# A fused attention and retention block on one core: parts of h by VectorE alone, reloads and stores at other steps

## The chip, the core and the metric

The kernel runs on one core of a Trainium2 chip. Its engines are TensorE (PE in the profile; PEld is its loading of weights), VectorE (DVE), ScalarE (ACT), GpSimd (POOL) and SyncE (SP), which only issues DMAs. ScalarE and GpSimd issue DMAs too, from their own queues. Each engine works off its instructions in the order of the program. The metric is device time in microseconds of one execution.

## The reference

One layer of an encoder over 512 positions and 2048 channels, all in float32. Cut to what matters here:

```
h    = rmsnorm(x) * norm_gain
proj = h @ w_in          # split into aq ak av az | iq ik iw | rq rk rv rz | ga gb
sel  = top 256 of relu(iq . ik) weighted by iw, per query, chunk-causal
a    = softmax(aq . ak[sel] * s + bias[bucket(pos)]) @ av[sel] * silu(az)
b    = groupnorm(retention(rope(rq), rope(rk), rv)) * silu(rz)
m    = sigmoid(ga) * (a @ w_a_out) + sigmoid(gb) * (b @ w_b_out)
r    = x + m @ w_o
y    = rmsnorm(r + (p @ w_ple) * sigmoid(r @ w_ple_gate)) * final_gain
```

## The kernel before

Every matrix product is made precise by splitting each operand into a high part (a copy to fp32r) and a low part (the rest), and adding three products: high x high, high x low, low x high. For a weight, `split_to` does this: ScalarE writes the high part `wh` (L153) and, one or more steps later, VectorE the low part `wl` (L158). Weights come from HBM into `wraw`, or into one of five big buffers (`wt`), by DMAs on SP's queue (`load_to`, L132), eight units ahead of use; they are split three units ahead.

Most projections are done in pairs with seven products in place of eight (a Strassen-like scheme). It needs sums of weight blocks: the sum of two blocks is made by loading one and letting a second DMA add the other in place (`add_block`, L119; it is issued on GpSimd's queue, and waits there until the buffer may be changed). It also needs sums and differences of the four quarters of h. `combos` makes these: for each of eight k, `xn_norm` scales two tiles of x (L707), `sums` makes four differences of 256 columns (L313 to L316), and `parts` splits each of seven operands into a copy on ScalarE (L299) and a low part (L301, or L303 where the sign is turned). In the kernel before, the four differences and three of the seven low parts (s1, s4, a22) are GpSimd's, the rest VectorE's. Of the first four k, the last three operands (twelve tiles, `x_away`) are stored to HBM (`hd`) and loaded back by `x_load`, as there are not enough tile slots (69) while the plain parts of h are still needed.

Order is written out by hand. `step()` counts steps: one follows each three matmuls in the plain products, and each two in `gemm_pair`. A function can be put off by n steps (`later`), put in line (`todo`), or on a background list (`bg`), of which one entry is run each `rate` steps when nothing else is in line. The background list holds, in this order, the parts of h (a load, a norm and four steps for each k), 48 top-k rounds on VectorE (MAX8 and a replace over 256, 384 or 512 columns, L650 and L651, after the last round of each a mask, L653), and the relative bias: masks on VectorE (L666), two banks of matmuls at a time (`bias_mm`, L677), an eviction on ScalarE (L685) and stores to HBM (L689).

The program runs through: index projections and scores; the retention values rv in two halves of 64 steps (`values`, four accumulators, evicted by ScalarE at the end, L764, and stored from its queue, L892); the attention values in one pair (`values_pair`, seven products of 16 steps: banks v, p, q, r, p, v, p, shown as ps_vv, ps_vp and so on; its results leave through `value_out`, L899, L906); then eight heads of retention, each a pair for rq and rk followed by two pairs for gates; then the pairs for rz, for aq and ak, and for az, attention with the output of branch b beside it, and the output projections.

Of the kernel before, what the change touches and what calls it, by code (L numbers as in the profile page):

```python
# [9 lines left out]
F32 = mybir.dt.float32  # L10
F32R = mybir.dt.float32r
# [24 lines left out]
def block_kernel(tc, xT, pT, posb, posq, w_in, w_v, w_ik, w_a, w_b, w_o, w_ple, w_gate,  # L36
# [4 lines left out]
    with contextlib.ExitStack() as ctx:  # L41
# [29 lines left out]
        raw_tiles = {}  # L71
        unfinished = {}
        state = {"raw": 0, "split": 0, "rate": BG_RATE}
        in_raws, in_big = set(), set()

        def raw(src, k0, nk, cols, plus=None):
            raws.append((src, k0, nk, cols, plus))
# [60 lines left out]
        def split_to(n, lag=1):  # L138
            while state["split"] < min(n, len(units)):
                i = state["split"]  # L140
                load_to(i + 1)
                r, plus, nk, cols = units[i]
                if r in unfinished:
                    unfinished[r]()
                raw = view(raw_tiles[r], nk, cols)
                if i in in_raws:
                    t = wp.tile([128, 2, 512], F32R, name="whl", tag="wraw", bufs=RAW_BUFS)
                    h, l = t[:, 0:1], t[:, 1:2]
                elif nk * cols == L:
# [3 lines left out]
                act.activation(h, raw, AF.Copy)  # L153

                def rest(r=r, plus=plus, l=l, raw=raw, h=h):
                    if unfinished.pop(r, None) is None:
                        return
                    dve.tensor_sub(l, raw, h.bitcast(F32))  # L158
# [129 lines left out]
                if ended[n] == 16 and n in after:  # L288
                    after[n]()

        def combos(lo, hi, name, keep=None, adder=dve, low={}):


            X = {n: [None] * 8 for n in PRODUCTS}
            T = {}

            def parts(n, k, src, sign=1.0):
                t = U(name + n, F32R)
                act.activation(t[:, LO], src, AF.Copy, scale=sign)  # L299
                if sign > 0:  # L300
                    low.get(n, dve).tensor_sub(t[:, HI], src, t[:, LO].bitcast(F32))  # L301
                else:
                    dve.scalar_tensor_tensor(t[:, HI], src, sign, t[:, LO].bitcast(F32), op0=OP.mult, op1=OP.subtract)  # L303
# [318 lines left out]
        def index_tile(m, ix):  # L622
            if m > 1:
                todo.extend(N3)
            for s in range(2):
                for t in range(1, NT):
                    todo.append(lambda s=s, t=t: index_score(2 * m + s, ix[s], t))

        for m in range(2):
            index_tile(m, ix[m])  # L630
        for m in range(2, 8):
# [49 lines left out]
        def bias_out(b, ps):  # L681
            t, gs = b
            ln = 128 * (t + 1)
            e = U("bev")
            act.activation(e[:, :ln * len(gs)], ps[:, :ln * len(gs)], AF.Copy, scale=d_back)  # L685
            for n, g in enumerate(gs):
                dst = bass.AP(tensor=scr.tensor, offset=scr.offset + 16 * (g % 8) * 1280 + TOFF[t],
                              ap=[[1280, 16], [128 * 1280, NH], [1, ln]])
                later(8 + 4 * n, lambda dst=dst, n=n: sp.dma_start(dst, e[:, ln * n:ln * n + ln]))  # L689

        def bias_banks(banks):
            for b, ps in [(b, bias_mm(b)) for b in banks]:
                bias_out(b, ps)

        x_away = [(n, k) for k in range(X_AWAY) for n in PRODUCTS[4:]]
        hd = dp.tile([len(x_away), 128, L], F32, name="hd")
        x_at = {nk: hd[i] for i, nk in enumerate(x_away)}
        xn = {}

        def xn_load(k):  # L700
            for i in (k, k + 8):
                xn[i] = U("xn")
                sp.dma_start(xn[i], xT[:, i, :])

        def xn_norm(k):
            for i in (k, k + 8):
                dve.scalar_tensor_tensor(xn[i], xn[i], ng[:, i:i + 1], R["b"], op0=OP.mult, op1=OP.mult)  # L707

        Xh, h_step = combos(lambda k: xn[k], lambda k: xn[k + 8], "h", lambda n, k: x_at.get((n, k)), pool,
                            {n: pool for n in ("s1", "s4", "a22")})  # L710
        bg.append(lambda: xn_load(0))
        for k in range(8):
            if k < 7:
                bg.append(lambda k=k: xn_load(k + 1))
            bg.append(lambda k=k: xn_norm(k))
            bg.extend([lambda k=k, i=i: h_step(k, i) for i in range(X_STEPS)])

        bg.append(lambda: state.update(rate=BG_RATES[1]))
        for r in range(16):
            for t in range(1, NT):  # L720
                bg.append(lambda r=r, t=t: topk_round(t, r == 15))
        bg.append(lambda: state.update(rate=BG_RATES[4]))
# [170 lines left out]
        state["rate"] = BG_RATES[2]  # L893


        def value_out(i, t, f, x, y):

            a = U("av")
            f(a, x, y)  # L899
            if t == NT - 1:  # L900
                vs = [(6, a)]
            else:
                h, l = split(a, "av", 2)
                vs = [(2 * t, h.bitcast(F32)), (2 * t + 1, l.bitcast(F32))]
            for j, v in vs:
                later(10 + 2 * (j % 2), lambda j=j, v=v: act.dma_start(vd[i, j], v))  # L906

        def values_pair(ids):
            banks = {}
# [4 lines left out]
                for j in range(2):  # L914
                    act.activation(E[n][j], banks[b][j], AF.Copy)

            def out(f, b, n, i, half):
                for j in range(2):
                    value_out(i, 2 * half + j, f, banks[b][j], E[n][j])
# [14 lines left out]
            for n, b in enumerate("vpqrpvp"):  # L934
# [3 lines left out]
                for s, (i, k) in enumerate(seq):  # L938
                    if k == 0:
                        split_to(i + AHEAD)  # L940
                        load_to(i + AHEAD + LOADS)
                    h, l = loaded[i]
                    x = Xh[PRODUCTS[n]][s]
                    for j in range(2):
# [7 lines left out]
                    after[n]()  # L952

        values_pair(u_av)
        state["rate"] = BG_RATES[3]


        sgb, sga, mbs = (dp.tile([16, 128, L], F32, name=n) for n in ("sgb", "sga", "mbs"))
# [26 lines left out]
        state["rate"] = BG_RATES[5]  # L985
        for n, u in enumerate(u_rz):
            y = B("y2")

# [402 lines left out]
AHEAD = 3  # L1391
LOADS = 5
BG_RATE = 4
BG_RATES = (2, 3, 5, 24, 16, 8)
X_AWAY = 4
HEAD = 13
WARM = 10
MANUAL = True
# [96 lines left out]
```

## Time and profile before

| | |
|---|---|
| median of three runs | 1684.4 us (1682.68 to 1685.42) |
| the profiled execution | 1680.43 us, span 1678.7 us |
| granted clock of TensorE, mean | 0.998 |
| GpSimd busy from 148 to 192 us (second half of rv) | 35.41 of 44 us |
| VectorE busy there | 39.35 of 44 us |

A row of the timeline has the start in us, the duration in us, the engine (SPq or ACTq for a DMA issue), the line, the operation, out<-in with shapes, how many were merged into the row, and in brackets the idle time before it with what ended it. A row of a group has mean ns after its busy time.

### The profile page before, as it was taken

Reading aid. Unit: us, or ns where it says so; the run is one execution under the profiler, and the core shown is the slowest. Engines: PE = TensorE matmul, PEld = TensorE weight load, DVE = VectorE, ACT = ScalarE, POOL = GpSimd, SP = SyncE. Lnnn points to the kernel's source line nnn. Section 1 sums busy time; section 2 is a strip of 40 time slices with the busy share of each in tenths; the row PEclk is TensorE's granted clock in tenths of the full one; section 3 lists DMA queues with packets and bytes.
Section 4 is the critical chain, followed back from the end, with each engine's and each line's share of the span. In section 5 each row is a group of like instructions: output and inputs, shape, how many; then the busy total and the mean of one; then the engine's idle time right before and its main releaser. Section 6 shows DMA issues by size and latency. Waiting matters only on the chain.

```text
span 1678.7 us, 24639 instructions
## 1 busy us (share of the span) xinstructions
PE 1660.2 (99%) x9160; PEld 1441.5 (86%) x9160; DVE 1300.1 (77%) x1984; ACT 880.0 (52%) x1296; POOL 284.3 (17%) x288
## 2 busy tenths in 40 slices
PE   9999999999999999999999999999999999999997
PEld 7988788888888888888888888888888888888896
DVE  7798988988988887887887777787668887864453
ACT  7465544555555555555555555566633445463342
POOL 2116611111111111111331111100000111112222
PEclk9999999999999999999999999999999999999999
DMA  7427989788788788788998888898466788733222
GB/s 288 127 91 236 321 234 268 174 218 218 181 210 220 178 232 230 168 229 227 248 235 219 218 223 218 247 373 284 162 210 193 196 216 218 208 108 101 88 63 101
DMA packets 125577, 343.26 MB, mean 204 GB/s; under 512 B 13713, under 2 KB 25873, under 8 KB 125457
## 3 DMA queue, kind: packets, MB, share of 16 engines
q1 hardware_dynamic: 90400, 235.22, 41.5%
q0 software_dynamic: 23680, 85.99, 28.1%
q10 hardware_dynamic: 11376, 20.47, 3.4%
q8 instruction: 72, 1.18, 0.3%
q14 instruction: 49, 0.39, 0.1%
HBM read 300.21 MB, written 41.42 MB: 204 GB/s over the span
## 4 chain that ended last, share of the span: by engine, by line
PE 89%; DVE 4%; ACT 2%; issue 2%; POOL 2%; DMA 1%; ACTq 0%; SPq 0%; POOLq 0%; DVEq 0%
PE ps_p L283 23%; PE ps_v L283 15%; PE ps_r L283 8%; PE ps_q L283 7%; PE ps_w L213 3%; PE ps_w L214 3%; PE ps_w L215 3%; PE ps_pg L215 3%; PE ps_pg L213 3%; PE ps_pg L214 3%; PE ps_iq L213 1%; PE ps_iq L215 1%; PE ps_iq L214 1%; DVE wl L158 1%; ACT wh L153 1%
## 5 line engine op out<-in xcount | busy, mean ns | idle before, releaser
L158 DVE TENSOR_TENSOR wl<-wraw,wh 128x1024 fp32r<-128x1024 f32 (+2 forms) x459 | 565.4, 1241 | 156.6 <-ACT wh L153 155.4
L153 ACT ACTIVATE wh<-wraw 128x1024 fp32r<-128x1024 f32 (+2 forms) x459 | 474.3, 1043 | 257.9 <-DVE wraw L160 120.3
L119 POOL DMA_DIRECT2D wraw<-w_in x120 | 106.1, 962 | 644.1 <-DVE mk L666 245.3
L283 PE MATMUL ps_p<-hs,wh 128*128 128x512 f32 x640 | 161.1, 394 | 0.0
L246 ACT ACTIVATE e<-ps_p 128x512 f32<-128x512 f32 x144 | 86.1, 598 | 136.7 <-PE ps_p L283 134.3
L283 PEld LDWEIGHTS ps_p<-hs,wh 128*128 128x128 f32 x640 | 114.9, 189 | 21.3 <-issue 0.7
L283 PE MATMUL ps_p<-hs,wl 128*128 128x256 f32 x640 | 92.1, 284 | 1.6 <-DVE wl L158 1.6
L283 PEld LDWEIGHTS ps_p<-hs,wl 128*128 128x128 f32 x640 | 83.0, 192 | 2.1 <-DVE wl L158 2.0
L283 PE MATMUL ps_r<-hs,wh 128*128 128x512 f32 x320 | 79.9, 392 | 1.3 <-ACT wh L153 1.3
L119 POOL DMA_DIRECT2D wraw<-w_o x24 | 21.1, 945 | 348.5 <-DVE wl L158 316.5
L283 PE MATMUL ps_q<-ha,wh 128*128 128x512 f32 x320 | 80.1, 392 | 0.0
L283 PE MATMUL ps_v<-ha,wh 128*128 128x512 f32 x320 | 80.0, 392 | 0.0
L283 PE MATMUL ps_p<-ha,wh 128*128 128x512 f32 x320 | 79.3, 390 | 0.0
L283 PE MATMUL ps_v<-hs,wh 128*128 128x512 f32 x320 | 79.0, 389 | 0.0
L215 PE MATMUL ps_pg<-rh,wl 128*128 128x512 f32 x192 | 74.8, 390 | 0.0
L214 PE MATMUL ps_pg<-rl,wh 128*128 128x512 f32 x192 | 74.7, 389 | 0.0
L213 PE MATMUL ps_pg<-rh,wh 128*128 128x512 f32 x192 | 74.7, 389 | 0.0
L967 DVE TENSOR_TENSOR go<-e_t 128x256 f32<-128x256 f32 x160 | 68.0, 425 | 6.8 <-DMA bd<-go 1.2
L283 PEld LDWEIGHTS ps_r<-hs,wh 128*128 128x128 f32 x320 | 59.6, 188 | 15.8 <-ACT wh L153 2.9
L283 PEld LDWEIGHTS ps_p<-ha,wh 128*128 128x128 f32 x320 | 59.9, 188 | 12.9 <-issue 0.5
L283 PEld LDWEIGHTS ps_v<-hs,wh 128*128 128x128 f32 x320 | 60.1, 188 | 12.5
L283 PEld LDWEIGHTS ps_v<-ha,wh 128*128 128x128 f32 x320 | 59.5, 188 | 12.1
(409 smaller groups left out, 3739.9 us busy)
## 6 DMA issues: line engine op xcount, KB each, us to landing
wraw<-w_in SPq DMA_DIRECT2D x172, 512.0 KB, 5.3
wraw<-w_in POOLq DMA_DIRECT2D x120, 512.0 KB, 8.0
wraw<-w_v SPq DMA_DIRECT2D x32, 512.0 KB, 4.2
wraw<-w_o SPq DMA_DIRECT2D x32, 512.0 KB, 4.8
wraw<-w_o POOLq DMA_DIRECT2D x24, 512.0 KB, 7.0
wraw<-w_gate SPq DMA_DIRECT2D x24, 512.0 KB, 4.0
wraw<-w_b SPq DMA_DIRECT2D x16, 512.0 KB, 5.9
wraw<-w_a SPq DMA_DIRECT2D x16, 512.0 KB, 4.1
```

What stands on the lines that cost most here:

```text
L119: pool.dma_start(out=view(raw_tiles[r], nk, cols), in_=src[:, k0:k0 + nk, :], accum_op=OP.add)
L153: act.activation(h, raw, AF.Copy)
L158: dve.tensor_sub(l, raw, h.bitcast(F32))
L213: pe.matmul(o, h[:, k, w], a, start=(s == order[0]), stop=False)
L214: pe.matmul(o, h[:, k, w], b, start=False, stop=False)
L215: pe.matmul(o, l[:, k, w], a, start=False, stop=(s == order[-1]))
L246: act.activation(E[n], src, AF.Copy)
L283: pe.matmul(o[:, c], w[:, k], X[PRODUCTS[n]][k][:, c], start=(n < 4 and first and k == 0), stop=(ended[n] == 16), skip_group_check=True)
L967: dve.tensor_add(o[:, q], c0, c1)
```

## The change

All differences and low parts of h go to VectorE; the functions for them move up in the text. The twelve tiles come back at every second step from step 4 of the second half of rv on (`X_BACK`; six of them during the attention values) in place of twelve steps in a row. When the first product of the attention values has been split, the second block is added to its weight 24 steps later (`ADD_LAG`). The evictions of rv stand three steps apart. The results of the last two outputs of `values_pair` begin 2 to 16 steps later; three of them use big buffers for their two halves, whose low ones are stored from GpSimd's queue. The bias stores are issued from GpSimd's queue, 14 steps after the bank and not 8. Four empty entries follow the parts of h on the background list, and the rate of the top-k rounds, which was set to 3 and at the end of rv to 5, is only set to 5.

```diff
-        def combos(lo, hi, name, keep=None, adder=dve, low={}):
+        def combos(lo, hi, name, keep=None):
...
-                    low.get(n, dve).tensor_sub(t[:, HI], src, t[:, LO].bitcast(F32))
+                    dve.tensor_sub(t[:, HI], src, t[:, LO].bitcast(F32))
...
-                adder.tensor_sub(t2[:, LO], x[:, LO], x[:, HI])
-                adder.tensor_sub(t1[:, LO], x[:, HI], y[:, HI])
-                adder.tensor_sub(t1[:, HI], x[:, LO], t1[:, LO])
-                adder.tensor_sub(t2[:, HI], y[:, LO], t1[:, HI])
+                dve.tensor_sub(t2[:, LO], x[:, LO], x[:, HI])
+                dve.tensor_sub(t1[:, LO], x[:, HI], y[:, HI])
+                dve.tensor_sub(t1[:, HI], x[:, LO], t1[:, LO])
+                dve.tensor_sub(t2[:, HI], y[:, LO], t1[:, HI])
...
-                        add_block(r, plus)
+                        later(ADD_LAG if r in in_big and r not in added else 0, lambda: add_block(r, plus))
+                        added.add(r)
...
-                later(8 + 4 * n, lambda dst=dst, n=n: sp.dma_start(dst, e[:, ln * n:ln * n + ln]))
+                later(14 + 4 * n, lambda dst=dst, n=n: pool.dma_start(out=dst, in_=e[:, ln * n:ln * n + ln]))
...
-        Xh, h_step = combos(..., lambda n, k: x_at.get((n, k)), pool,
-                            {n: pool for n in ("s1", "s4", "a22")})
+        Xh, h_step = combos(..., lambda n, k: x_at.get((n, k)))
...
-        bg.append(lambda: state.update(rate=BG_RATES[1]))
+        bg.extend([lambda: None] * 4)
...
-            if s >= KT - len(x_away) and x_wanted:
+            if s in X_BACK:
...
-            pss = values(u_rv[i], "rv", x_load if i else lambda s: None)
-            for t, ps in enumerate(pss):
-                act.dma_start(rd[i, t], normal(ps, "rv", t))
+            for t, ps in enumerate(values(u_rv[i], "rv", x_load if i else lambda s: None)):
+                later(3 * t, lambda i=i, t=t, ps=ps: act.dma_start(rd[i, t], normal(ps, "rv", t)))
...
-                h, l = split(a, "av", 2)
-                vs = [(2 * t, h.bitcast(F32)), (2 * t + 1, l.bitcast(F32))]
-            for j, v in vs:
-                later(10 + 2 * (j % 2), lambda j=j, v=v: act.dma_start(vd[i, j], v))
+            later(lags[0], lambda: act.activation(h, a, AF.Copy))
+            later(lags[1], lambda: dve.tensor_sub(l, a, h.bitcast(F32)))
+            later(lags[2], lambda: store(2 * t, h.bitcast(F32)))
+            later(lags[2] + 4, lambda: store(2 * t + 1, l.bitcast(F32)))
...
-                out(dve.tensor_sub, "p", "pv", 1, 1)
-                out(dve.tensor_add, "r", "e3", 1, 0)
+                out(dve.tensor_sub, "p", "pv", 1, 1, (2, 6), (6, 9, 22), True)
+                out(dve.tensor_add, "r", "e3", 1, 0, (10, 16), (6, 9, 22), True)
...
+                    x_load(KT + 8 * n + s)
...
+ADD_LAG = 24
+X_BACK = (4, 6, 8, 10, 12, 14, 22, 24, 26, 28, 30, 32)
```

More of the change, by code (lines that the diff above doesn't have):

```diff
@@ L73, in block_kernel @@
         state = {"raw": 0, "split": 0, "rate": BG_RATE}
-        in_raws, in_big = set(), set()
+        in_raws, in_big, added = set(), set(), set()
         def raw(src, k0, nk, cols, plus=None):
@@ L627, in index_tile, with xn_load, xn_norm, x_steps @@
                     todo.append(lambda s=s, t=t: index_score(2 * m + s, ix[s], t))
+        x_away = [(n, k) for k in range(X_AWAY) for n in PRODUCTS[4:]]
+        hd = dp.tile([len(x_away), 128, L], F32, name="hd")
+        x_at = {nk: hd[i] for i, nk in enumerate(x_away)}
+        xn = {}
+        def xn_load(k):
+            for i in (k, k + 8):
+                xn[i] = U("xn")
+                sp.dma_start(xn[i], xT[:, i, :])
+        def xn_norm(k):
+            for i in (k, k + 8):
+                dve.scalar_tensor_tensor(xn[i], xn[i], ng[:, i:i + 1], R["b"], op0=OP.mult, op1=OP.mult)
+        Xh, h_step = combos(lambda k: xn[k], lambda k: xn[k + 8], "h", lambda n, k: x_at.get((n, k)))
+        def x_steps(k):
+            load = [lambda: xn_load(k + 1)] if k < 7 else []
+            return load + [lambda: xn_norm(k)] + [lambda i=i: h_step(k, i) for i in range(X_STEPS)]
         for m in range(2):
@@ L693, in bias_banks @@
                 bias_out(b, ps)
[L695 to L709, printed above, removed]
-                            {n: pool for n in ("s1", "s4", "a22")})
+        rounds = [lambda r=r, t=t: topk_round(t, r == 15) for r in range(16) for t in range(1, NT)]
         bg.append(lambda: xn_load(0))
         for k in range(8):
[L713 to L716, printed above, removed]
-        bg.append(lambda: state.update(rate=BG_RATES[1]))
[L719 to L722, printed above, removed]
+            bg.extend(x_steps(k))
+        bg.extend([lambda: None] * 4)
+        bg.extend(rounds)
+        bg.append(lambda: state.update(rate=BG_RATES[3]))
         banks = [(t, tuple(range(8 * t + g, 8 * t + g + n))) for t, n in reversed(tuple(enumerate((4, 2, 1, 1))))
@@ L889, in block_kernel, with value_out, store @@
         for i in range(2):
-            pss = values(u_rv[i], "rv", x_load if i else lambda s: None)
-            for t, ps in enumerate(pss):
-                act.dma_start(rd[i, t], normal(ps, "rv", t))
-        state["rate"] = BG_RATES[2]
-        def value_out(i, t, f, x, y):
-            a = U("av")
+            for t, ps in enumerate(values(u_rv[i], "rv", x_load if i else lambda s: None)):
+                later(3 * t, lambda i=i, t=t, ps=ps: act.dma_start(rd[i, t], normal(ps, "rv", t)))
+        state["rate"] = BG_RATES[1]
+        def value_out(i, t, f, x, y, lags, big=False):
+            def store(j, v):
+                (pool if big and j % 2 else act).dma_start(out=vd[i, j], in_=v)
+            if big and t < NT - 1:
+                b = B("avhl", F32R)
+                a, l, h = b[:, 0:L].bitcast(F32), b[:, 0:L], b[:, L:2 * L]
+            else:
+                a = U("av")
             f(a, x, y)
             if t == NT - 1:
-                vs = [(6, a)]
-            else:
-                h, l = split(a, "av", 2)
-                vs = [(2 * t, h.bitcast(F32)), (2 * t + 1, l.bitcast(F32))]
-            for j, v in vs:
-                later(10 + 2 * (j % 2), lambda j=j, v=v: act.dma_start(vd[i, j], v))
+                return later(lags[2], lambda: store(6, a))
+            if not big:
+                h, l = U("avh", F32R), U("avl", F32R)
+            later(lags[0], lambda: act.activation(h, a, AF.Copy))
+            later(lags[1], lambda: dve.tensor_sub(l, a, h.bitcast(F32)))
+            later(lags[2], lambda: store(2 * t, h.bitcast(F32)))
+            later(lags[2] + 4, lambda: store(2 * t + 1, l.bitcast(F32)))
         def values_pair(ids):
@@ L915, in copy, with out @@
                     act.activation(E[n][j], banks[b][j], AF.Copy)
-            def out(f, b, n, i, half):
+            def out(f, b, n, i, half, at=(0, 0), *rest):
                 for j in range(2):
-                    value_out(i, 2 * half + j, f, banks[b][j], E[n][j])
+                    later(at[j], lambda j=j: value_out(i, 2 * half + j, f, banks[b][j], E[n][j], *(rest or ((2, 3, 10),))))
             def last():
                 copy("e3", "p")
-                out(dve.tensor_sub, "p", "pv", 1, 1)
-                out(dve.tensor_add, "r", "e3", 1, 0)
+                out(dve.tensor_sub, "p", "pv", 1, 1, (2, 6), (6, 9, 22), True)
+                out(dve.tensor_add, "r", "e3", 1, 0, (10, 16), (6, 9, 22), True)
             after = {
```

6 lines of the change are left out of this document (3 added, 3 removed).

## Prediction

> **What bounds the kernel now.** I read the page first, then the table of waits for TensorE alone, then the busy times of three stretches around the last value projections.
>
> ```profile
> span 1678.7 us, 24639 instructions
> ...
> PE 1660.2 (99%) x9160; PEld 1441.5 (86%) x9160; DVE 1300.1 (77%) x1984; ACT 880.0 (52%) x1296; POOL 284.3 (17%) x288
> ```
>
> TensorE is the bound: everything else can only matter where it makes TensorE wait. Not one matmul is added or removed, so the most that can be won is the waiting. Who it waits for:
>
> ```profile
> PE ps_b L1368 <- POOL rl L1364: 3.5, 1, 3.5
> PE ps_p L283 <- DVE wl L158: 1.6, 2, 1.3
> PE ps_vv L948 <- DVE wl L158: 1.5, 2, 0.8
> PE ps_vv L947 <- ACT wh L153: 1.4, 1, 1.4
> ...
> PE ps_r L283 <- ACT wh L153: 1.3, 3, 0.6
> ```
>
> The first row lies in the kernel's tail, which the change leaves alone. The other four are 5.8 us, all waits for the two halves of a weight (wh from ScalarE, wl from VectorE). They are too small as they stand, since a matmul's end is modelled: it is shown for longer than the pace at which the next can follow. The count per stretch shows the real loss.
>
> ```profile
> 148.00:192.00 44.00, 44.00 (x196) 36.44 (x195) 39.35 (x37) 22.02 (x44) 35.41 (x39) 1.00 0.92 292
> 192.00:202.00 10.00, 7.07 (x29) 4.98 (x28) 6.54 (x12) 7.76 (x12) 5.01 (x7) 1.00 1.06 344
> 202.00:246.00 44.00, 44.00 (x196) 36.41 (x195) 38.28 (x64) 19.67 (x22) 4.13 (x6) 1.00 0.85 244
> ```
>
> Columns: length, then busy us (and instructions) of PE, PEld, DVE, ACT, POOL, then clock, DMA share, GB/s. Before and after, 196 matmuls pass in 44 us, 0.2245 us each; in the 10 us between there are 29 instead of 44.5. So 15.5 x 0.2245 = **3.5 us** are lost there, the largest single loss. What happened in it:
>
> ```profile
> 192.98 1.04 ACT L153 ACTIVATE wh<-wt 128x1024 fp32r<-128x1024 f32 x1
> ...
> 194.54 0.67 ACT L764 ACTIVATE rv<-ps_vn,r_nat 128x512 f32<-128x512 f32 x1
> ...
> 194.59 1.21 DVE L158 TENSOR_TENSOR wl<-wt,wh 128x1024 fp32r<-128x1024 f32 x1
> ...
> 195.73 0.41 DVE L650 MAX8 m<-isc 128x8 f32<-128x256 f32 x1
> ...
> 195.86 0.50 PE L948 MATMUL ps_vv<-wl,hs 128*128 128x512 f32 x1 [0.79 <-DVE wl L158]
> ...
> 197.87 0.69 ACT L764 ACTIVATE rv<-ps_vn,r_nat 128x512 f32<-128x512 f32 x1 [0.48 <-POOL hs L301]
> ...
> 198.97 2.01 ACT L153 ACTIVATE wh<-wt 128x1024 fp32r<-128x1024 f32 x2 [0.40 <-ACT rv L764]
> ...
> 200.07 0.50 PE L947 MATMUL ps_vv<-wh,hs 128*128 128x512 f32 x1 [1.38 <-ACT wh L153]
> ...
> 201.33 0.50 PE L948 MATMUL ps_vv<-wl,hs 128*128 128x512 f32 x1 [0.76 <-DVE wl L158]
> ```
>
> Two causes. The second weight's wl (194.59) is late because VectorE is still at the parts of h. The third's wh (198.97) is late because four evictions of rv, each followed by its DMA issue, stand in one row on ScalarE's queue from 194.54 to 198.97, 4.4 us.
>
> **Parts of h by VectorE alone.** In the second stretch of this work VectorE and GpSimd run side by side:
>
> ```profile
> L158 DVE TENSOR_TENSOR wl<-wraw,wh 128x1024 fp32r<-128x1024 f32 x5 | 10.1, 2024 | 0.0
> L707 DVE SCALAR_TENSOR_TENSOR xn<-xn,g_sb,r_b 128x512 f32<-128x512 f32 x8 | 8.5, 1095 | 0.0
> L301 DVE TENSOR_TENSOR hs<-t,hs 128x256 fp32r<-128x256 f32 x7 | 6.6, 959 | 0.0
> ```
>
> And once, for the first k, they don't (VectorE's rows; then GpSimd's, idle for 11.18 us before 123.84; then VectorE at a time when GpSimd only issues DMAs):
>
> ```profile
> 116.98 0.42 DVE L303 SCALAR_TENSOR_TENSOR ha<-xn,ha 128x256 fp32r<-128x256 f32 x1
> ...
> 117.65 0.41 DVE L301 TENSOR_TENSOR hs<-t,hs 128x256 fp32r<-128x256 f32 x1
> ...
> 123.84 0.91 POOL L301 TENSOR_TENSOR hs<-t,hs 128x256 fp32r<-128x256 f32 x1 [11.18 <-ACT hs L299]
> ...
> 134.56 1.41 DVE L707 SCALAR_TENSOR_TENSOR xn<-xn,g_sb,r_b 128x512 f32<-128x512 f32 x2
> ```
>
> ```profile
> L158 DVE TENSOR_TENSOR wl<-wraw,wh 128x1024 fp32r<-128x1024 f32 x17 | 20.7, 1220 | 4.2 <-ACT wh L153 4.1
> ```
>
> So beside GpSimd's work a half of 256 columns takes VectorE 0.96 us, alone 0.41; a wl 2.02 and 1.22; a pair of xn 2.19 and 1.41. The change moves 7 of 11 small operations per k to VectorE. Alone, one k costs 1.41 + 11 x 0.41 = 5.9 us. The stretch 148 to 192 is the second half of rv: 64 steps of 0.69 us, in which the background list reaches five k's (six entries each, one entry every second step) and eight wl. That gives 5 x 5.9 + 8 x 1.22 = 39.3 us of VectorE, against 39.35 busy now: seven more operations per k for no more busy time, as the waiting on GpSimd goes. Records of neighbours overlap (116.98 and 117.65 are two operations, 0.34 apart each), so the true demand is nearer 5 x (1.3 + 11 x 0.34) + 8 x 1.14 = 34.5. Either is below 44, and a weight is split three units ahead of its use, so VectorE's queue need not run late at 192. ScalarE, whose copies wait for GpSimd's sums in the same chain (0.48 at 197.87 is one), is freed as well. The late wl at 194.59 goes.
>
> **Evictions of rv three steps apart** go between the splits on ScalarE's queue instead of ahead of them: the third wh is then behind one eviction (1.1 us with its issue), not four. TensorE idled 1.38 us for it (200.07); three evictions less are 3.3 us. The later add of sum's second block takes four DMA issues, which wait for a wl, out of this place; they are due only when the fifth product is split, some 40 steps on. The moved half of the twelve reloads of h is due as late. Bytes are the same in all of these. I put the whole 3.5 us here as won (bounds 1.5 to 3.5).
>
> **Last values.** The loss at 283:
>
> ```profile
> 278.32 2.81 ACTq L906 DMA_DIRECT2D vd<-avl  x3
> ...
> 281.18 0.60 ACT L246 ACTIVATE pv<-ps_v 128x512 f32<-128x512 f32 x1 [3.38 <-DVE wl L158]
> ...
> 283.24 1.23 DVE L158 TENSOR_TENSOR wl<-wraw,wh 128x1024 fp32r<-128x1024 f32 x1 [2.99 <-ACT wh L153]
> ...
> 284.52 0.74 PE L283 MATMUL ps_p<-hs,wl 128*128 128x256 f32 x4 [1.30 <-DVE wl L158]
> ```
>
> ScalarE's queue stands 2.8 us at three store issues, its copies and the next wh come late, VectorE idles 2.99 us for that wh, TensorE 1.30 for wl; with the modelled end of the matmul before (about 0.16) **1.5 us**. In the changed kernel the four outputs start 2 to 16 steps later, their stores 22 to 26 steps after that, and the low halves leave from GpSimd's queue. Won: 1.5 (bounds 0 to 1.5: an operation moved back could meet the next wh).
>
> **Heads of retention.** Four more waits (three for wh, one for wl):
>
> ```profile
> 301.16 0.74 PE L283 MATMUL ps_r<-hs,wh 128*128 128x512 f32 x2 [0.62 <-ACT wh L153]
> ...
> 364.29 0.50 PE L283 MATMUL ps_r<-hs,wh 128*128 128x512 f32 x1 [0.27 <-ACT wh L153]
> ...
> 489.83 0.73 PE L283 MATMUL ps_r<-hs,wh 128*128 128x512 f32 x2 [0.40 <-ACT wh L153]
> ...
> 492.27 0.69 DVE L650 MAX8 m<-isc 128x8 f32<-128x512 f32 x1
> ...
> 493.78 0.43 DVE L653 TENSOR_SCALAR mneg<-isc 128x512 bf16<-128x512 f32 x1
> ...
> 495.39 0.50 PE L283 MATMUL ps_p<-hs,wl 128*128 128x256 f32 x2 [0.33 <-DVE wl L158]
> ```
>
> With 0.16 each for modelled ends they cost 2.3 us. VectorE's queue carries a top-k round into each. Counted through the background list, after the values the changed kernel stands two rounds further back at the same step (four empty entries stand ahead of the rounds now), so each of these places gets another length: 512 columns (0.69 for the MAX8) become 256 (0.41), 256 become 384, 384 become 512. The place at 495 gets the short one, the one at 364 too, the other two a longer one; and the delay carried on from 283 is gone at 301. I take 1.1 of the 2.3 as won (bounds 0.5 worse to 2.3 better).
>
> **Bias stores.** 32 stores leave SP's queue for GpSimd's. Both queues are slack; GpSimd's holds the accumulating loads. The nearest row is its plain store of a tile (shortest, median and longest in ns); then who waited for the accumulating loads, us and times:
>
> ```profile
> L992 POOL DMA_DIRECT2D bd<-go x8: 607/608/617, 802.1 to 868.3; - x8
> ```
>
> ```profile
>   ACT wh L153: 11.6, 6
> ```
>
> 32 x 0.61 = 20 us for an engine that loses 56 operations of about 0.91 (123.84), 51 us. They come in 11 groups of two to eight, now 14 steps after their bank instead of 8, so that the eviction is done when GpSimd's queue reaches them. Behind a pair of them stands at worst an accumulating load, 1.2 us later; and these loads have made ScalarE wait 11.6 us in six places, while among TensorE's waits none is for a load. Cost 0 (bounds 0 to 1.2 a group, 13 in all).
>
> **Sum.** 3.5 + 1.5 + 1.1 = 6.1 us. The profiled execution took 1680.4 (1678.7 of span and 1.7 around it), so it would be 1674.3. Its own time is 4.0 below the median of the runs, 1684.4; the loss is the same in both, and I forecast the median: **1678.3 us**, 0.36% less. About 0.2%, 3.4 us, is what a measurement can tell here.
>
> **Rivals.**
> *Values alone* (0.14): the 3.5 us go, the rest is reshuffled, 1680.9. For it: the waits at the heads come from queues that keep their load. It lies on the limit, so I count half as faster.
> *Moved, not gone* (0.08): VectorE, with seven more operations per k, reaches 192 as late as now; 1684.4. For it: 39.3 us by one of my sums is no less than today's busy time. Against: today's lateness came through a chain over three engines.
> *The price stays* (0.05): the 0.96 comes from something other than GpSimd, such as DMA traffic (292 GB/s there). Then 5 x 7 x 0.96 = 34 us are added to 39 in 44; with some 9 us of lead from the splits ahead, 20 us reach TensorE, 1704. Against: at 244 GB/s wl takes 1.22, and VectorE is slow only where GpSimd's sums stand beside it.
> *Bias stores in front of loads* (0.07), the slower side: if TensorE pays for every pair of stores, 11 x 1.2 = 13 us come on top, 1684.4 - 6.1 + 13.4 = 1691.7. It decides from 0.55 us a group on. [...]
>
> **Numbers.** Forecast 0.66. Faster by over 0.2%: 0.66 + 0.07 = 0.73; within: 0.07 + 0.08 = 0.15; slower: 0.05 + 0.07 = 0.12. The range leaves out the two slow rivals. Upper end: nothing won, and the highest run shown lay 1.0 above its median: 1685.4. Lower end: all 7.3 us won and the 4.0 us by which the profiled execution lies under the median: 1673.1.
>
> **What would show it.** The rows of ps_vv and the 1.30 at 283 leave TensorE's waits; the ten microseconds after the second half of rv hold about 44 matmuls; L301 on VectorE means about 0.41, wl about 1.22 in that stretch; GpSimd loses 56 sums. It is wrong if ps_vv still waits for wl, if VectorE's halves stay near 0.9, or if a new wait for an accumulating load shows after 550.

## The result, and the profile after

| | before | changed |
|---|---|---|
| median | 1683.24 us (1682.11 to 1685.42, 6 runs) | 1674.07 us (1672.95 to 1674.74, 6 runs) |
| profiled execution | 1680.43 us, span 1678.7 us | 1672.95 us, span 1671.2 us |

The ratio is 0.9943, with a 95% interval of 0.9931 to 0.9956: 9.2 us faster. The two profiled executions differ by 7.5 us. That these two numbers are not the same is part of the story below.

The page of the changed kernel, span and engines:

```profile
span 1671.2 us, 24606 instructions
...
PE 1658.4 (99%) x9160; PEld 1441.6 (86%) x9160; DVE 1293.6 (77%) x2040; ACT 878.3 (53%) x1296; POOL 249.9 (15%) x267
```

VectorE has 56 operations more and is busy 6.5 us less; GpSimd is busy 34 us less, although it issues 32 stores more. Whom TensorE waited for (us, times, longest), from the longest down to 0.6:

```profile
PE ps_b L1376 <- POOL rl L1372: 3.5, 1, 3.5
PE ps_warm L408 <- DVE warm L403: 1.4, 1, 1.4
PE ps_r L284 <- ACT wh L153: 0.6, 2, 0.3
```

The rows of ps_vv and ps_p are gone; of the heads of retention two waits of 0.3 are left. The same stretches as before the change (length; busy us and instructions of PE, PEld, DVE, ACT, POOL; clock, DMA share, GB/s):

```profile
148.00:192.00 44.00, 44.00 (x196) 36.45 (x195) 37.30 (x77) 24.57 (x51) 5.45 (x6) 1.00 1.00 304
192.00:202.00 10.00, 10.00 (x46) 8.29 (x45) 6.44 (x10) 5.88 (x7) 1.75 (x2) 1.00 1.06 300
202.00:246.00 44.00, 44.00 (x196) 36.45 (x195) 36.66 (x60) 20.65 (x23) 4.69 (x6) 1.00 0.87 258
```

The ten microseconds after the second half of rv hold 46 matmuls and not 29. In the 44 before them VectorE runs 77 operations in place of 37, in less busy time, and GpSimd 5.45 us in place of 35.41. VectorE's groups there (us 160 to 192; busy us, mean ns):

```profile
L302 DVE TENSOR_TENSOR hs<-t,hs 128x256 fp32r<-128x256 f32 x16 | 5.9, 419 | 0.0
L158 DVE TENSOR_TENSOR wl<-wraw,wh 128x1024 fp32r<-128x1024 f32 x4 | 4.9, 1226 | 2.3 <-ACT wh L153 2.3
L642 DVE SCALAR_TENSOR_TENSOR xn<-xn,g_sb,r_b 128x512 f32<-128x512 f32 x6 | 4.2, 745 | 0.0
```

A half of 256 columns went from 959 to 419 ns, a wl from 2024 to 1226, an xn from 1095 to 745, as forecast (0.41, 1.22, and 1.41 for a merged pair). The bias stores on GpSimd's queue (ns shortest, median, longest), and, from another answer, who waited for the accumulating loads (us, times):

```profile
L710 POOL DMA_DIRECT2D scr<-bev x32: 532/785/1171, 568.0 to 1062.8; - x32
```

```profile
  ACT wh L153: 16.5, 11
```

A bias store takes 0.79 us at the median, where the plain store of a tile before the change took 0.61. The bias masks on VectorE are not the reason: the nine stores that overlap a mask have a median of 0.58 us, the other 23 one of 0.83. ScalarE waits for accumulating loads more often (16.5 us in 11 places, before 11.6 in 6); none of it reaches TensorE.

To place the gain I took, for each pair of neighbouring matmuls of a trace, the time from start to start less the median for that shape. Summed by place, in us ("loss" from here on):

| place | before | changed | won | forecast |
|---|---|---|---|---|
| 190 to 206 us (attention values begin) | 3.8 | 0.0 | 3.8 | 3.5 |
| about 280 (first product of retention) | 1.5 | 0.0 | 1.5 | 1.5 |
| heads of retention | 0.79 + 0.43 + 0.56 + 0.49 | 0.50 + 0.17 + 0.44 | 1.2 | 1.1 |
| first 104 us and the tail, untouched | 6.4 | 5.7 | 0.7 | 0 |

That is 7.2 of the 7.5 us.

### The profile page after: what moved, and what is told of

Read it like the earlier page. It is cut to its first block, busy times and chain, and to the rows that moved or that the text cites. A ratio compares the mean times of both kernels' runs of the same rounds, so it can differ in the third digit from the quotient of the medians.

```text
span 1671.2 us, 24606 instructions
## 1 busy us (share of the span) xinstructions
PE 1658.4 (99%) x9160; PEld 1441.6 (86%) x9160; DVE 1293.6 (77%) x2040; ACT 878.3 (53%) x1296; POOL 249.9 (15%) x267
## 4 chain that ended last, share of the span: by engine, by line
PE 95%; DVE 2%; ACT 2%; issue 1%; DMA 0%; POOL 0%; SPq 0%; POOLq 0%; ACTq 0%; DVEq 0%
PE ps_p L284 24%; PE ps_v L284 16%; PE ps_r L284 8%; PE ps_q L284 8%; PE ps_w L214 3%; PE ps_w L215 3%; PE ps_w L216 3%; PE ps_pg L216 3%; PE ps_pg L214 3%; PE ps_pg L215 3%; PE ps_vn L755 2%; PE ps_vn L757 2%; PE ps_vn L756 2%; PE ps_iq L214 1%; PE ps_iq L216 1%; PE ps_iq L215 1%
```

## The experiments

Loss is by the same count throughout. The first four ran beside 24 runs of the kernel before on the same chip (median 1683.1), the next four beside 6 (1681.71), the next three beside 10 (1681.12), the last beside 11 (1681.3). The kernel before itself moves by 2 us from group to group, so times of different groups can be compared only to within that.

**All parts of h on VectorE, alone.** The kernel before with one edit:

```diff
-        Xh, h_step = combos(..., pool, {n: pool for n in ("s1", "s4", "a22")})
+        Xh, h_step = combos(...)
```

> The kernel before with one edit: all sums and low parts of h on VectorE. Theory 1 (GpSimd's sums slow VectorE's operations, and their chain makes the second weight's wl late): between 160 and 192 us VectorE's small halves mean 0.42 us and wl 1.22; the wait for the second wl (0.95 us of loss) is gone, and the four evictions start some 2.5 us earlier, so that of the other 2.6 us about 1 is left: 2.5 us faster than before. Rival (the price of 0.96 comes from DMA traffic, or VectorE becomes the bound): halves stay above 0.8 us and the kernel is 10 to 20 us slower. Rival (the four evictions alone made the loss): 0 to 1 us faster.

Measured: 1678.48 us, ratio 0.9983 (0.9969 to 0.9997). The waits of ps_vv are gone altogether, not all but 1 us. About 280 us 0.85 is lost, at the heads of retention 2.3, as before the change. Three of the ten runs, all with a mean granted clock of 0.995, took 1682.78 us or more, the others 1676.05 to 1679.05.

**The evictions of rv three steps apart, alone.** The kernel before with one edit:

```diff
-            pss = values(u_rv[i], "rv", x_load if i else lambda s: None)
-            for t, ps in enumerate(pss):
-                act.dma_start(rd[i, t], normal(ps, "rv", t))
+            for t, ps in enumerate(values(u_rv[i], "rv", x_load if i else lambda s: None)):
+                later(3 * t, lambda i=i, t=t, ps=ps: act.dma_start(rd[i, t], normal(ps, "rv", t)))
```

> The kernel before with one edit: the evictions of rv three steps apart. Theory 1 (two causes side by side): the wait for the second wl (0.95 us) stays, the waits for the third wh and wl (2.6 us) mostly go: about 2 us faster. Rival (the evictions alone are the cause): 3.5 us faster. Rival (the chain over GpSimd is the cause of both): 0 to 0.5 us faster.

Measured: 1677.87 us, ratio 0.9971 (0.9961 to 0.9981). These waits of ps_vv are gone here too, and that with GpSimd at its sums as ever. The two stretches, and VectorE's groups from 160 to 192:

```profile
148.00:192.00 44.00, 44.00 (x196) 36.44 (x195) 42.20 (x40) 24.55 (x49) 37.26 (x41) 1.00 1.01 312
192.00:202.00 10.00, 10.00 (x46) 8.29 (x45) 9.76 (x16) 6.19 (x8) 4.09 (x5) 1.00 1.05 344
```

```profile
L158 DVE TENSOR_TENSOR wl<-wraw,wh 128x1024 fp32r<-128x1024 f32 x4 | 7.9, 1980 | 0.4 <-ACT wh L153 0.4
L301 DVE TENSOR_TENSOR hs<-t,hs 128x256 fp32r<-128x256 f32 x8 | 7.4, 958 | 0.0
```

VectorE is as slow as before the change, and TensorE has its 46 matmuls. But VectorE is busy 42.20 of the 44 us, where it was 39.35: the slow operations alone made no wait, it had been late as well. Where the lateness came from stands some 45 us earlier, at the first half's evictions. Timeline of the kernel before, rows of ScalarE and VectorE:

```profile
147.98 0.67 ACT L764 ACTIVATE rv<-ps_vn,r_nat 128x512 f32<-128x512 f32 x1
...
152.33 1.06 ACT L153 ACTIVATE wh<-wraw 128x1024 fp32r<-128x1024 f32 x1 [0.40 <-ACT rv L764]
153.43 1.23 DVE L158 TENSOR_TENSOR wl<-wraw,wh 128x1024 fp32r<-128x1024 f32 x1 [4.07 <-ACT wh L153]
```

The same in the kernel with spaced evictions:

```profile
149.32 1.06 ACT L153 ACTIVATE wh<-wraw 128x1024 fp32r<-128x1024 f32 x1 [0.46 <-ACT rv L764]
...
150.41 1.22 DVE L158 TENSOR_TENSOR wl<-wraw,wh 128x1024 fp32r<-128x1024 f32 x1 [0.85 <-ACT wh L153]
```

Four evictions in a row held the wh back to 152.33, and VectorE, in whose queue the wl stands ahead of all further parts of h, idled 4.07 us. With one eviction ahead of it the wh starts at 149.32 and the idling is 0.85. Those 3.2 us are nearly what VectorE is busy more in the 44 (2.85), and what its chain lacked at 192: the second weight's wl, at 194.59 in the kernel before, starts here at 191.59, when the first eviction of the second half has only just begun.

```profile
191.54 0.67 ACT L764 ACTIVATE rv<-ps_vn,r_nat 128x512 f32<-128x512 f32 x1
...
191.59 1.21 DVE L158 TENSOR_TENSOR wl<-wt,wh 128x1024 fp32r<-128x1024 f32 x1
```

So these 3.0 us come from the first half's spacing alone. The lateness needs the slow operations to become a wait: with all parts of h on VectorE it idles 4.50 us at 154.09, and nothing is late at 192. One share is not shown. The edit spaces the second half's evictions too, and no run spaces the first half's alone. An estimate from the rows: four evictions in a row from 191.54, 4.4 us as before, would put the third weight's wh at 196.0 and its wl at 197.1 to 198.3; here TensorE first uses that wl at 197.84, so about 0.4 us of waiting would be left. This profile also has a wait that no other has, 1.13 us for a wl at 836.02 (1.8 of loss with the matmuls behind it); its cause is open.

**Both together.** The two edits above on the kernel before.

> The kernel before with both edits, nothing else: sums and low parts on VectorE, evictions three steps apart. If these two are the whole of the first gain, the ten microseconds after the second half of rv hold some 44 to 46 matmuls, the waits of ps_vv are gone, and the kernel is 3.5 us faster than before, with the wait at 283 us (1.5 us) and those at the heads as before. If the later reloads and the later second add are needed too, ps_vv still waits for 0.5 us or more.

Measured: 1678.22 us, ratio 0.9973 (0.9963 to 0.9983). No more than either alone: the two do not add up, each removes the same wait. About 280 us 1.29 is lost.

**The last values as before.** The changed kernel with the old start and lags of the last four outputs, and the old lag of the low halves' stores:

```diff
-            later(lags[2] + 4, lambda: store(2 * t + 1, l.bitcast(F32)))
+            later(lags[2] + 2, lambda: store(2 * t + 1, l.bitcast(F32)))
...
-                out(dve.tensor_sub, "p", "pv", 1, 1, (2, 6), (6, 9, 22), True)
-                out(dve.tensor_add, "r", "e3", 1, 0, (10, 16), (6, 9, 22), True)
+                out(dve.tensor_sub, "p", "pv", 1, 1)
+                out(dve.tensor_add, "r", "e3", 1, 0)
```

> The changed kernel with one edit undone: the last values leave at once, all from ScalarE's queue, in small tiles, as before. Theory 1 (ScalarE's queue stood at three store issues): a wait of ps_p for wl of about 1.3 us comes back near 279 us, and the first head waits 0.3 to 0.5 us more; 1.5 to 2 us slower than the changed kernel, 1675.8 against 1674.1. Rival (the earlier gain had already freed the queues there): no such wait, 1674.1.

Measured: 1677.28 us, ratio 0.9969 (0.9957 to 0.998), 3.2 us above the changed kernel's median. Timeline:

```profile
275.03 2.62 ACTq L898 DMA_DIRECT2D vd<-avl  x3
...
277.69 0.60 ACT L247 ACTIVATE pv<-ps_v 128x512 f32<-128x512 f32 x1 [4.02 <-issue]
...
281.04 1.21 PE L284 MATMUL ps_p<-hs,wl 128*128 128x256 f32 x8 [1.10 <-DVE wl L158]
```

The three store issues and the wait for wl are back: 1.26 us lost there, 0.6 more at the first head of retention, 0.3 at 431 us. That is 2.2; the count does not place the rest of the 3.2 in these stretches.

**GpSimd's sums back.** The changed kernel with `adder` and `low` in `combos` again, and GpSimd in them.

> The changed kernel with one edit undone: GpSimd makes the four differences and three low parts again. The first runs showed that VectorE alone, and the spaced evictions alone, each take the whole wait of ps_vv away. If that holds, this one has VectorE's halves at 0.96 us and wl near 2 us between 160 and 192 us again, but no wait of ps_vv: within 1 us of the changed kernel, 1674 to 1675. Rival (the sum of my prediction, each edit its own share): the wait for the second wl is back, 1 us or more, 1675 to 1678.

Measured: 1672.98 us (1672.82 to 1674.42), ratio 0.9951 (0.9933 to 0.9968). VectorE's groups from 160 to 192:

```profile
L158 DVE TENSOR_TENSOR wl<-wraw,wh 128x1024 fp32r<-128x1024 f32 x4 | 7.9, 1976 | 0.4 <-ACT wh L153 0.4
L302 DVE TENSOR_TENSOR hs<-t,hs 128x256 fp32r<-128x256 f32 x8 | 7.2, 923 | 0.2 <-ACT hs L300 0.2
```

VectorE runs at the old, slow durations, and no wait of ps_vv shows. In the changed kernel the edit that names the change is worth nothing that these runs can measure.

**Add and reloads at the old steps.** The changed kernel with ADD_LAG = 0 and the twelve reloads in steps 4 to 15 in a row.

> The changed kernel with the DMA timing undone: the twelve tiles come back at steps 4 to 15 in a row, and the second block is added as soon as its buffer may be changed. My prediction put these at nothing: 1674 to 1674.5, no new wait of TensorE in the values. Rival (they carry a part of the gain, since the DMA engines are full there): a wait for wh or wl of 0.5 to 3 us between 190 and 285 us, 1674.5 to 1677.

Measured: 1673.69 us, ratio 0.9953 (0.9935 to 0.9971), no new wait. Worth nothing.

**Bias stores on SP's queue.** The changed kernel with one line:

```diff
-                later(14 + 4 * n, lambda dst=dst, n=n: pool.dma_start(out=dst, in_=e[:, ln * n:ln * n + ln]))
+                later(8 + 4 * n, lambda dst=dst, n=n: sp.dma_start(out=dst, in_=e[:, ln * n:ln * n + ln]))
```

> The changed kernel with the bias stores on SP's queue, 8 steps after the bank, as before. My prediction put this part at nothing: 1674, and no wait of TensorE between 550 and 1090 us in either. Rival (the stores stood in front of the weights on SP's queue and cost TensorE something): 1 to 3 us slower. Rival (GpSimd's queue is the worse place): 0.5 us or more faster.

Measured: 1673.14 us, ratio 0.995 (0.9934 to 0.9966). Worth nothing in time, at this place in the program. The waits are not quite as expected: at 751.73 TensorE waits 0.38 us for state (0.55 of loss), as a wh at 749.16 had waited 2.51 us for its load. Whether the stores on SP's queue made that load late is not shown.

**The kernel before, a second profile.** Unchanged, for what differs between its executions.

> The kernel before, unchanged, for a second profile: its timed runs lie between 1679 and 1684 us, its profiled execution at 1680.4. If its waits differ from one execution to the next, this profile shows other sizes of the waits at 195 to 201 and at 283 us, and the difference of the two profiles lies in these places. If the spread comes from elsewhere (the start, the end, the pace of matmuls), these waits are the same to 0.2 us.

Measured: 1683.59 us, span 1681.8, 3.2 us above the first profile and 0.4 from the median of 1683.24. Windows:

```profile
192.00:202.00 10.00, 7.06 (x29) 5.00 (x28) 6.58 (x10) 7.69 (x12) 4.96 (x7) 0.99 1.05 347
202.00:205.00 3.00, 3.00 (x8) 2.33 (x8) 2.93 (x7) 0.30 (x1) 1.54 (x2) 0.50 1.02 281
205.00:246.00 41.00, 41.00 (x182) 33.96 (x181) 34.44 (x57) 19.32 (x21) 2.96 (x5) 1.00 0.82 236
```

In the ten microseconds the same 29 matmuls. Then, though TensorE waits for nothing, only 8 matmuls in 3 us and not 15: the granted clock is 0.50. Eight neighbouring starts lie 0.427 us apart in place of 0.227, 1.6 us in all. The other difference is about 280 us. Timeline:

```profile
282.52 2.40 ACTq L906 DMA_DIRECT2D vd<-avl  x3
...
287.03 1.23 DVE L158 TENSOR_TENSOR wl<-wraw,wh 128x1024 fp32r<-128x1024 f32 x1 [4.14 <-ACT wh L153]
...
288.31 1.22 PE L283 MATMUL ps_p<-hs,wl 128*128 128x256 f32 x8 [2.59 <-DVE wl L158]
```

The same chain as in the first profile, with 4.14 us of idling in place of 2.99, and 2.59 us of waiting in place of 1.30. With a wait at 281 that was not there, 1.8 us more are lost here. These two are 3.4; what differs elsewhere, at the start, the heads and the tail, takes 0.2 back.

**Two edits for the whole.** The kernel before with the spaced evictions and the new last values (their big buffers and lags as in the change), nothing else.

> The kernel before with two edits of the change only: the evictions of rv three steps apart, and the last value outputs as the changed kernel has them. GpSimd keeps its sums, the second add of sum, the reloads of h and the bias stores stay as before. Theory (these two edits are the whole gain but the heads): no wait for a weight between 190 and 206 us, none at about 280; the four waits at the heads of retention as before, about 0.8, 0.4, 0.6 and 0.5 us lost, 2.3 in all against 1.1 in the changed kernel; so about 1.2 us slower than the changed kernel, 1674.5 to 1675.5, with a granted clock of at least 0.997 in every run. Rival (VectorE alone, or the DMA queues, must also give way for the last values): a wait of over 0.5 us stays at about 280, and 1676 to 1678.

Measured: 1674.1 us (1672.94 to 1675.13), ratio 0.9952 (0.9934 to 0.997). Nothing is lost from 190 to 206 us nor about 280; 0.27 is lost at 255, for a wl; at the heads 0.63, 0.45, 0.57 and 0.50, nearly as before. With the changed kernel's other parts left out the time is 0.4 below the expected band and the changed kernel's own to 0.1 us. Against the runs of the kernel before beside them, though, this kernel gains 7.0 us, the changed one 9.2, and the three kernels above that lack one of its parts 8.0 to 8.7. So these two edits carry the gain to within a microsecond or two; the 1 us at the heads in the count of the traces is less than the medians resolve.

**Three empty entries instead of four,** and **five**, ahead of the top-k rounds in the changed kernel:

```diff
-        bg.extend([lambda: None] * 4)
+        bg.extend([lambda: None] * 3)
```

> The changed kernel with three empty entries instead of four ahead of the top-k rounds, so every background entry after the values comes one entry earlier. Theory (the length of the top-k round that stands on VectorE's queue at the end of a retention head's first pair sets that head's wait: 256 columns about 0, 384 about 0.17, 512 about 0.45 to 0.5 us): the heads that saw 512, 256, 384 and 512 columns (0.50, 0, 0.17, 0.44 us lost) now see 256, 384, 512 and 256, so about 0, 0.2, 0.45 and 0 to 0.1: 0.7 in all instead of 1.1, 0 to 0.5 us faster than the changed kernel. Rival (the waits belong to the places, not to the rounds): 0.50, 0, 0.17 and 0.44 stay where they are.

> The changed kernel with five empty entries instead of four, so every background entry after the values comes one entry later. Theory as in the run with three: the heads now see 384, 512, 256 and 384 columns, so about 0.17, 0.45, 0 and 0.17 us lost, 0.8 in all instead of 1.1. Rival: 0.50, 0, 0.17 and 0.44 stay where they are. Neither moves the time by more than 0.5 us, so the place of the waits decides, not the time.

Measured: three 1675.66 us (1674.43 to 1678.86), ratio 0.9966 (0.9953 to 0.998); five 1673.57 (1673.33 to 1673.88), 0.9949 (0.9932 to 0.9967). The loss at each head, with the columns of the last round before it, read from its MAX8 row:

| head at about | three entries | four (changed kernel) | five |
|---|---|---|---|
| 295 | 256: 0.23 | 512: 0.50 | 384: 0.29 |
| 357 | 384: 0.17 | 256: 0 | 512: 0.44 |
| 420 | 512: 0.44 | 384: 0.17 | 256: 0 |
| 483 | 256 and mask: 0.52 | 512: 0.44 | 384: 0.16 |

One place in two kernels, the head at 357. The changed kernel:

```profile
347.68 0.42 DVE L671 MAX8 m<-isc 128x8 f32<-128x256 f32 x1
...
357.71 1.55 PE L284 MATMUL ps_r<-hs,wh 128*128 128x512 f32 x6
```

With five entries:

```profile
348.12 0.69 DVE L671 MAX8 m<-isc 128x8 f32<-128x512 f32 x1
...
358.58 1.65 PE L284 MATMUL ps_r<-hs,wh 128*128 128x512 f32 x6 [0.27 <-ACT wh L153]
```

The wait goes with the round, not with the place: 0, 0.17, 0.44 for 256, 384, 512 columns. Two things miss: the first head adds up to 0.2, and a round that ends with the mask (L674) costs as much as the longest. So three entries lose 1.5 us at the heads (0.17 of it in one more wait at 489) where 0.7 was expected, five 0.9 where 0.8 was.

What was not expected is the kernel with three entries: it is slower than the other two by 1.6 and 2.1 us. Its timeline, rows of GpSimd, ScalarE and TensorE:

```profile
1059.39 2.40 POOL L710 DMA_DIRECT2D scr<-bev  x4
...
1064.61 0.90 POOL L119 DMA_DIRECT2D wraw<-w_in  x1 [2.81 <-issue]
...
1074.50 2.00 ACT L153 ACTIVATE wh<-wraw 128x1024 fp32r<-128x1024 f32 x2 [5.94 <-DMA wraw<-w_in]
...
1075.61 0.88 PE L284 MATMUL ps_v<-hs,wh 128*128 128x512 f32 x2 [2.12 <-ACT wh L153]
```

Four bias stores stand ahead of this accumulating load, and four more ahead of the one before it. In the changed kernel each of the two loads stands ahead of its group:

```profile
1060.65 0.94 POOL L119 DMA_DIRECT2D wraw<-w_in  x1 [2.59 <-issue]
1061.25 2.44 POOL L710 DMA_DIRECT2D scr<-bev  x4
```

This load starts there at 1060.65, four microseconds sooner. With three entries the data come late, ScalarE idles 5.94 us and TensorE 2.12. After the wait, in its windows:

```profile
1064.00:1073.00 9.00, 9.00 (x57) 8.09 (x56) 3.39 (x4) 2.35 (x3) 0.90 (x1) 1.00 1.00 297
1073.00:1076.00 3.00, 0.88 (x5) 0.41 (x4) 0.41 (x1) 1.50 (x2) 0.00 (x0) 1.00 0.81 301
1076.00:1079.00 3.00, 3.00 (x9) 2.31 (x8) 2.96 (x4) 1.19 (x3) 0.86 (x1) 0.51 0.13 16
```

The clock is halved again, 0.51, right behind a wait: 2.3 us lost by the wait and 1.4 by the clock. The profiled run is the only one of the seven with a mean clock of 0.997, the others have 0.998, so the clock's part may be this run's alone.

**Three entries, bias stores on SP's queue.** The kernel with three entries and the one line of the run with the stores on SP's queue.

> The changed kernel with three empty entries instead of four, as in the run before, and the bias stores back on SP's queue, 8 steps after their bank. In the run with three entries and the stores on GpSimd's queue TensorE waited 2.1 us at 1073 us for the wh of an accumulated weight, and its clock was halved for some 3 us after it. Theory (four bias stores, 2.4 us, and the wait in front of them stood on GpSimd's queue ahead of that weight's accumulating load, issued at 1064.6 us instead of 1060.7 in the changed kernel): the wait at 1073 and the halved clock are gone, the heads of retention wait as in the run with three, and the time is 2 to 4 us less than there: about 1673 to 1674. Rival (the load is late for the entry's place alone, whatever queue the stores are on, as GpSimd's sequencer waits for the wl ahead of it): the wait of about 2 us stays, and 1675 to 1677.

Measured: 1676.28 us (1675.48 to 1678.59), ratio 0.9969 (0.9959 to 0.998). The wait at 1073 is gone, as the theory had it, but the time is no better, since another came. Timeline, rows of SP, GpSimd, ScalarE and TensorE:

```profile
951.60 3.80 SPq L710 DMA_DIRECT2D scr<-bev  x4
...
955.50 13.87 SPq L132 DMA_DIRECT2D wraw<-w_in  x7
...
966.62 0.88 POOL L119 DMA_DIRECT2D wraw<-w_in  x1 [10.61 <-issue]
...
975.70 2.01 ACT L153 ACTIVATE wh<-wraw 128x1024 fp32r<-128x1024 f32 x2 [5.94 <-DMA wraw<-w_in]
...
976.81 0.50 PE L284 MATMUL ps_v<-hs,wh 128*128 128x512 f32 x1 [2.12 <-ACT wh L153]
```

On SP's queue the four stores stand ahead of the plain load that the accumulating one has to follow, and TensorE waits 2.12 us at 976, with no halved clock behind it. The theory missed the time; the rival, which expected the wait at 1073 to stay, had the time right and the reason wrong. What follows: with the bias one entry sooner, a group of stores meets a load on either queue. For the wait at 1073 the run itself shows that moving the stores to SP's queue, 8 steps after the bank, takes it away; for the one at 976 the order on the queue is read from the rows, as no run took these stores away.

## Why the prediction was right, and where it was not

**What bounds the kernel.** Right: all that was won is waiting of TensorE for wh and wl, at the places named.

**Parts of h by VectorE alone.** The durations came as forecast (419, 1226, 745 ns), and the rival "The price stays" is refuted: the 0.96 us did come from GpSimd's sums, as the runs with and without them show (0.42 against 0.92 to 0.96), with the DMA engines as full in both (share 1.00 in the changed kernel, 1.01 with the evictions alone). By what way GpSimd's sums slow VectorE is not shown. The share of this edit in the 3.5 us, though, was wrong. I gave it the late wl (194.59) and the evictions the late wh. The runs show that either edit alone removes both, and that with the evictions spaced the sums may stay on GpSimd. The reason is a step that I did not take: I read the evictions at 194.54 and not those of the first half at 147.98, which had put VectorE back by 3 us before its slow stretch began. The sum for VectorE in the 44 us comes to 34.3 by its own terms and not 34.5; it was busy 37.30, between that and the 39.3.

**Evictions.** Right in size (3.5 forecast, 3.8 in the count), in the main by a longer way than I gave: 3.2 of the 4.07 us of idling at 153.43 taken away. What the spacing at 194.54, which I had in mind, adds to that is not shown; the estimate above makes it some 0.4 us.

**Last values.** Right in the profile (1.5), but the term is no constant. It was 1.5 and 3.4 in two profiles of the kernel before, and 0.85, 2.21 and 1.29 in the three partial kernels, each time behind three store issues that took 2.4 to 3.6 us of ScalarE's queue. Their length alone does not set it, as the loss of 3.4 went with 2.40 us, the shortest. Taken out of the changed kernel this edit costs 3.2 us, of which the count places 2.2.

**Heads.** 1.1 forecast, 1.2 measured, and that the wait goes by the length of the round is now shown at these heads (0, 0.17 and 0.44 us for 256, 384 and 512 columns). My bounds (0.5 worse to 2.3 better) held: with three and five entries 1.5 and 0.9 us are lost there.

**Bias stores, add, reloads at nothing.** Right for the changed kernel, each by a run. The slower rival, "Bias stores in front of loads", is a real mechanism all the same, and 2.3 to 3.7 us at one place in the runs with three entries. I had it decided by the price of a pair of stores; it is decided by which side of an accumulating load a group falls on, and in the changed kernel it falls on the good side by one entry. No run shows that VectorE's bias masks lengthen a store: the stores that overlap a mask are not the longer ones (0.58 us against 0.83), one store of the kernel before, at 868.34, also overlapped a mask and took 0.61, and the kernels with three entries wait on either queue.

**The sum.** 6.1 us forecast; 7.5 in the profiles, of which 0.7 lies where nothing was changed; 9.2 in the medians. The step that failed is "the loss is the same in both": I took the 4.0 us between the profiled execution and the median for a part that the change doesn't touch. The second profile shows what it is there: 1.6 us of halved clock right after the waits that the change removes, and 1.8 us of a longer wait about 280. The measured 1674.07 is 4.2 below my forecast, and lies inside the range only because I took these 4.0 us off its lower end, though my sum held them to be untouched.

How often the clock drops, the mean granted clock of a run tells only in part. In four profiles the last 5.5 to 8.8 us run at half clock (the kernel before 7.9 and, in its second profile, 5.5, the changed kernel 6.9, all parts on VectorE 8.8), which alone makes a mean of 0.997 or 0.998, and all fourteen profiles have such a mean; the profile with the drop at 202 has 0.997, and so have three whose clock is 1.00 from 202 to 205. A mean that is shown as 0.996 or less is 0.35% or more below full speed, 5.9 us of the span; the end, at half clock for 8.8 us at most in those four, explains up to 4.4 of them. By this estimate such a run has at least about one drop more. Of 51 runs of the kernel before, 20 had 0.995 or 0.996 and took 1682.78 to 1685.91 us; 14 had 0.998 and took 1678.72 to 1682.9, with a median of 1680.1, which is 6.0 us above the changed kernel and about the sum that I worked out. The changed kernel's six had 0.997 or 0.998, as did all with both big waits gone. That the drops of the other runs follow these waits is inferred: one profile shows it, and the kernel with all parts on VectorE, where ps_vv waits for nothing, had 0.995 in three of its ten runs.

## What to carry to other kernels

Look for a late chain's cause where it was last on time, not where it waits: here four evictions in a row cost nothing on the spot and, together with VectorE's slow operations, most of 3.8 us some forty-five microseconds later, and moving one function a few steps did what a redistribution of work over two engines also did. Where TensorE is the bound, a wait can cost more than its length: in two profiles here the clock was halved right after waits, for 1.6 and 1.4 us more. So compare the profiled execution with the median, and profile twice where they differ. An edit that costs nothing because of where it lands (the bias stores) should be tried one step to each side before it is called free.

## What the runs showed of the hardware that was not expected

- The clock was halved after waits of TensorE that were short, but not after each of them: for 3.4 us after three within 6 us (0.78, 1.40 and 0.76 us) in one profile of the kernel before, and not in the other, with 0.79, 1.38 and 0.76; for 3.4 us after a single one of 2.12 us in one kernel (1075.61), and not in another (976.81). At the 3.52 us wait of ps_b near the end it was halved in the kernel before from 1670.8 us on, 0.3 before the wait was over, and in the changed kernel from 1664.3 on, 0.4 after it, and stayed so to the end. What decides whether a wait brings the drop is not shown.
- A store issue of 0.33 us (the issues of rv) took 0.8 to 1.2 each, on the mean, for three in a row about 280 us (2.40 to 3.59 for three), and ScalarE's next work stood behind them. The DMA engines were busy throughout (share 0.98 to 1.06), but so they were from 192 to 202 us (1.06), where the issues of rv kept their 0.33, each some 1.1 us after the last. So full DMA engines alone do not explain it; the cause is open.
